# A planner that writes the instruction order by hand: accumulator reads by two engines counted one behind the other, and a larger backlog bound

## The chip, the cores and the metric

The kernel runs on one core of a Trainium2 chip. The metric is device time in microseconds (us) of one execution. Five engines work side by side: TensorE (PE in the profile; its weight loads are PEld), VectorE (DVE), ScalarE (ACT), GpSimd (POOL) and SyncE (SP), which issues most DMAs. Every engine executes its own instructions in the order in which the program issued them.

## The reference

One layer of a decoder for 512 prompt tokens and 8 x 4 sample tokens, all in one matrix of 544 columns, model width 1024, in float32:

```python
hp = _ffn_half(hp, ...)                      # x + 0.5 * SwiGLU(RMSNorm(x)), hidden width 2816
q, k, v, u, gv = _in_proj(_rmsnorm(hp), w_in)  # 8 x 64 | 2 x 64 | 2 x 64 | 512 | 512
q = _rope(q, pos_p)
k = _rope(k, pos_p)
ya = _swa_prompt(q, k, v, sinks)             # window of 128, sinks, blocks of 128 queries
yg = _gmlp(u, gv, ws, b_s)                   # gelu(u) * (tril(W_s) @ RMSNorm(gelu(gv)) + b)
hp = hp + concat(_rmsnorm(ya), _rmsnorm(yg)) @ w_out
hp = _ffn_half(hp, ...)
y = _rmsnorm(hp)
```

The sample tokens take the same path, with attention over a cache of 128 keys each. The last keys, values and gating rows are outputs too.

## The kernel before

Activations lie transposed: 128 features on the partitions, 544 tokens along the free dimension. Each float32 operand is split into a high part (rounded to fp32r) and a low part (the remainder), and a product is three fp32r matmuls: high x high, high x low, low x high. A matmul has 272 columns, half of the tokens. Weights stream in by DMA as `raw` tiles; ScalarE makes the high part `wh`, VectorE the low part `wl`.

Stages in order of time: the first feed-forward block (tiles `aga`, `aua`, `pa_`, `ada`), then the mixing stage in `mix`, then the second feed-forward block (`agb`, `aub`, `pb_`, `adb`) with the final norm. In the mixing stage TensorE's main work is 14 projection tiles of 48 matmuls, in the order k, q0, q1, v, g0, q2, g1, q3, g2, g3, u0 to u3 (accumulators `zk`, `zq`, `zv`, `zg`, `zu`), and then the output projection `o` in two halves of eight tiles: the first needs the attention's result, the second the gating's. Two accumulators turn by turn, with a third one at times, take the tiles.

The other work is side work: Python generators that are advanced in between. They are `unit` (eight attention units of four heads by 128 queries: scores `sp`, softmax in `so`, transposes `tp` to `PT`, product `po`; units 0 to 3 need q0 and q1, units 4 to 7 need q2 and q3), `samples` (`sps`, `srow`, `tps`, `pos`), `outs` (transposes `tpv`, `tpk` of v and k, and their stores), `turn_gv` (transposes `tg`), `y_gen` and `a_stat` (the attention's norm, `R_a`), and `gmlp` (the gating: Gelu of `gv` and `u`, products `mp`, its norm `R_g`). `gmlp` is marked late. In a unit, each `yield` names the tiles and flags that the next piece needs.

The order is written by the program itself, while it is built, with an estimate of time. `Model.put` keeps a clock for each engine (`t`) and, for each tile, a log of accesses with their end times. An instruction starts at the latest of its engine's clock, the accesses that its reads wait for, and the accesses that its writes wait for. `when(box, writes, eng)` gives the end of the latest overlapping access by another engine: with `writes=True` that of writes alone, with `False` that of reads and writes. The estimated costs of each operation are in `Model.op`; for a VectorE operation on two tensors of 544 elements it is 150 + 1.09 x 544 = 743 ns.

After every step of a projection (six matmuls, an eighth of a projection tile) `tick` looks for side work. It returns at once if VectorE's or ScalarE's clock is more than `BACKLOG` ahead of TensorE's. Otherwise it takes the first generator of the list that is `ready`, that is, whose operands are done by TensorE's clock and whose accumulators are free, and advances it until something is issued on TensorE. Late work is taken only where both clocks are less than `BACKLOG / 3` ahead. `force` advances side work without regard to the clocks until a flag is set; the program calls it where the main work needs the side work's result.

An accumulator is read by two engines in the evacuation of k and q, `ev_z`: ScalarE copies it in four pieces into `rot`, and VectorE reads it for `zc` (for k the tile is `kT`). The final norm reads one accumulator (`pRf`) on ScalarE and VectorE too.

```python
for b in range(4):
    nc.scalar.copy(g2(rot[b * 32:(b + 1) * 32, :]), ac[(b ^ 1) * 32:(b ^ 1) * 32 + 32, :, :HT])
zc = kT if kind == "k" else t544(f"zc{i}")
nc.vector.tensor_tensor(g2(zc), ac[:, :, :HT], g2(CR), op=ALU.mult)
nc.vector.tensor_tensor(rot, rot, SR, op=ALU.mult)
```

These two engines' instructions have the framework's semaphores between them; the model's clocks set only in which order the program issues the instructions, and, in `scale`, which of the two engines does a copy.

Of the kernel before, what the change touches and what calls it, by code (L numbers as in the profile page):

```python
# [10 lines left out]
PSUM = bass.MemoryType.PSUM  # L11
# [22 lines left out]
W_BUFS = 5  # L34
NX = 14
SLACK = 4500.0
BACKLOG = 2500.0
MARGIN = 0.0


class Model:
# [22 lines left out]

    def put(self, eng, ns, reads, writes, lat=100.0):
        two = [r for r in reads if len(r.ap) > 1 and r.ap[-1][1] > 1]
        reads, writes = [self.box(r) for r in reads], [self.box(w) for w in writes]
        t = max([self.t[eng]] + [self.when(r, True, eng) for r in reads] + [self.when(w, False, eng) for w in writes])
        if eng == "DVE" and sum(r.space != PSUM for r in two) == 2 and self.pool[0] <= t < self.pool[1]:
            t = self.pool[1]  # L70
        if eng == "POOL":
            self.pool = (t, t + ns)
        self.t[eng] = t + ns - {"DVE": 85.0, "ACT": 95.0}.get(eng, 0.0)
        for bs, w in ((reads, False), (writes, True)):
            for key, *b in bs:
                old = self.log.get(key, [])
                if w:
                    old = [e for e in old if not (b[0] <= e[0] and e[1] <= b[1] and b[2] <= e[2] and e[3] <= b[3])]
                self.log[key] = old[-60:] + [(*b, t + ns + lat, w, eng)]
# [66 lines left out]
class Prog:  # L146
# [34 lines left out]
    def tick(self):  # L181
        if max(self.m.t["DVE"], self.m.t["ACT"]) > self.m.t["PE"] + BACKLOG:
            return
        t = self.m.t["PE"]
        while self.m.t["PE"] == t:
            idle = max(self.m.t["DVE"], self.m.t["ACT"]) < t + BACKLOG / 3
            g = next((g for g in self.side if self.ready(g) and (idle or not g[2])), None)
            if g is None:
                return
            self._advance(g)  # L190
# [1433 lines left out]
```

## Time and profile before

| | us |
|---|---|
| median of 3 runs | 961.84 |
| lowest, highest run | 960.1, 968.4 |
| profiled execution, its own time | 960.9 |
| its span, first to last instruction | 959.2 |
| TensorE busy in the span | 939.2 |
| VectorE busy | 731.0 |
| ScalarE busy | 412.0 |

The mean granted clock of TensorE is 0.992 of full speed. Times in the profile count from the span's start. In the rows of instructions, the first two numbers are start and length in us; `out<-in` names tiles, with buffer numbers left out; `xN` merges N instructions; a bracket gives the idle time of the engine before the instruction and what ended it. Nearly all instructions have line L132, because one helper issues them: they are told apart by their tiles.

### The profile page before, as it was taken

What the parts mean: (1) busy time and instruction counts of PE and PEld (TensorE: products, weight loads), DVE (VectorE), ACT (ScalarE), POOL (GpSimd) and SP (SyncE); (2) the same over time, 40 slices, a digit from 0 to 9 for tenths busy, and PEclk for the clock granted to TensorE, in tenths of its full rate; (3) what the DMA queues carried; (4) which work ended last, traced back from release to release, by engine and by line L of the source; (5) the groups of instructions that cost most, each with busy time, mean ns of one, the idle gap of its engine ahead of it and who ended that gap; (6) DMA issues with size and microseconds to landing.
All of it is one profiled execution on the core that took longest, in us unless ns stands there. A gap on an engine that the chain in (4) does not pass through costs nothing.

```text
span 959.2 us, 18038 instructions
## 1 busy us (share of the span) xinstructions
PE 939.2 (98%) x7463; PEld 927.1 (97%) x7463; DVE 731.0 (76%) x1316; ACT 412.0 (43%) x655; POOL 46.0 (5%) x55
## 2 busy tenths in 40 slices
PE   8999999999999999999999999999999999999996
PEld 7999999999999999989999999999999999999996
DVE  6689996689668957586767796799966799745864
ACT  7434453243424436556546354334442344412432
POOL 0000000000000000130004300000000000000002
PEclk9999999999999999999999999999999999999998
DMA  7321225122422246231131222303242222512202
GB/s 250 121 78 44 90 93 169 65 82 72 144 82 89 77 144 207 67 95 45 67 106 54 73 71 95 104 25 109 78 144 89 87 90 88 177 45 89 88 2 93
DMA packets 29826, 90.86 MB, mean 95 GB/s; under 512 B 3808, under 2 KB 7248, under 8 KB 29600
## 3 DMA queue, kind: packets, MB, share of 16 engines
q1 hardware_dynamic: 28416, 87.85, 28.2%
q0 software_dynamic: 784, 1.30, 0.4%
q8 instruction: 58, 0.95, 0.4%
q10 hardware_dynamic: 544, 0.56, 0.2%
q14 instruction: 24, 0.20, 0.1%
HBM read 86.98 MB, written 3.74 MB: 95 GB/s over the span
## 4 chain that ended last, share of the span: by engine, by line
PE 89%; DVE 5%; ACT 3%; DMA 1%; issue 1%; SPq 0%; POOL 0%; DVEq 0%
PE ada L132 14%; PE adb L132 14%; PE o L132 3%; PE aub L132 3%; PE zu L132 2%; PE agb L132 2%; PE aga L132 2%; PE zg L132 2%; PE aua L132 2%; PE zq L132 1%; DMA x<-x 1%; PE pb_40P L132 1%; PE pa_121P L132 1%; PE pb_161P L132 1%; PE pa_40P L132 1%; PE pa_61P L132 1%
## 5 line engine op out<-in xcount | busy, mean ns | idle before, releaser
L132 ACT ACTIVATE wh<-raw 128x1024 fp32r<-128x1024 f32 (+2 forms) x240 | 220.3, 940 | 262.4 <-DVE raw L132 154.6
L132 DVE TENSOR_TENSOR wl<-raw,wh 128x1024 fp32r<-128x1024 f32 (+2 forms) x240 | 255.6, 1077 | 9.0 <-ACT wh L132 8.7
L132 PE MATMUL adb<-hhb,wh 128*128 128x272 f32 x352 | 78.5, 289 | 0.7 <-DVE hpb L132 0.7
L132 PE MATMUL adb<-hlb,wh 128*128 128x272 f32 x352 | 78.0, 288 | 0.9 <-DVE hlb L132 0.9
L132 PE MATMUL adb<-hhb,wl 128*128 128x272 f32 x352 | 78.1, 288 | 0.0
L132 DVE TENSOR_TENSOR raw<-raw,raw 128x512 f32<-128x512 f32 x108 | 74.2, 687 | 1.3
L132 PE MATMUL ada<-hha,wh 128*128 128x272 f32 x352 | 73.0, 289 | 0.9 <-ACT wh L132 0.9
L132 PE MATMUL ada<-hla,wh 128*128 128x272 f32 x352 | 72.7, 288 | 0.0
L132 PE MATMUL ada<-hha,wl 128*128 128x272 f32 x352 | 72.6, 288 | 0.0
L132 DVE SCALAR_TENSOR_TENSOR x<-adb,x 128x272 f32<-128x272 f32 x64 | 25.9, 436 | 46.8 <-PE adb L132 46.7
L132 PEld LDWEIGHTS adb<-hlb,wh 128*128 128x128 f32 x352 | 57.3, 189 | 1.2 <-DVE hlb L132 1.2
L132 PEld LDWEIGHTS adb<-hhb,wh 128*128 128x128 f32 x352 | 57.4, 188 | 0.9 <-DVE hpb L132 0.9
L132 DVE SCALAR_TENSOR_TENSOR x<-ada,x 128x272 f32<-128x272 f32 x64 | 25.2, 435 | 42.6 <-PE ada L132 42.6
L132 PEld LDWEIGHTS adb<-hhb,wl 128*128 128x128 f32 x352 | 57.1, 189 | 0.0
L132 PEld LDWEIGHTS ada<-hha,wh 128*128 128x128 f32 x352 | 55.2, 188 | 1.1 <-issue 1.1
L132 PEld LDWEIGHTS ada<-hla,wh 128*128 128x128 f32 x352 | 55.4, 189 | 0.0
L132 PEld LDWEIGHTS ada<-hha,wl 128*128 128x128 f32 x352 | 55.2, 189 | 0.0
L132 ACT ACTIVATE hhb<-hpb 128x544 fp32r<-128x544 f32 (+1 forms) x24 | 14.8, 621 | 39.5 <-DVE hpb L132 39.5
L132 ACT ACTIVATE hha<-hpa 128x544 fp32r<-128x544 f32 x22 | 14.5, 659 | 39.2 <-DVE hpa L132 39.2
L132 ACT ACTIVATE xh<-x,cols 128x544 fp32r<-128x544 f32 x24 | 17.8, 749 | 30.4 <-DVE x L132 27.2
L132 PE MATMUL o<-xh,wh 128*128 128x272 f32 x128 | 29.7, 298 | 0.6 <-DVE oa L132 0.6
L132 PE MATMUL o<-xl,wh 128*128 128x272 f32 x128 | 28.5, 289 | 0.1
(818 smaller groups left out, 2821.3 us busy)
## 6 DMA issues: line engine op xcount, KB each, us to landing
raw<-wgu SPq DMA_DIRECT2D x86, 512.0 KB, 3.9
raw<-wd SPq DMA_DIRECT2D x32, 384.0 KB, 3.5
raw<-wd SPq DMA_DIRECT2D x20, 512.0 KB, 4.7
raw<-win SPq DMA_DIRECT2D x14, 512.0 KB, 4.3
raw<-wout SPq DMA_DIRECT2D x8, 512.0 KB, 3.8
x<-x SPq DMA_DIRECT2D x8, 272.0 KB, 4.7
y<-x SPq DMA_DIRECT2D x6, 272.0 KB, 2.4
raw<-wgu SPq DMA_DIRECT2D x8, 128.0 KB, 3.7
```

The costliest lines, as they stand in the source:

```text
L132: return f(*args, **kw)
```

## The change

In `Model.put` a read of an accumulator (a tile in PSUM) now waits, in the estimate, for the reads of it by other engines as well as for the writes. Reads of other memory wait for writes alone, as before. And `BACKLOG` rises from 2500 to 5500 ns, which raises the bound for late work, a third of it, from 833 to 1833 ns. No instruction is added or removed by the edit itself. The order of side work in between the main work can differ, and which engine does the copies that `scale` places.

```diff
-BACKLOG = 2500.0
+BACKLOG = 5500.0
...
         two = [r for r in reads if len(r.ap) > 1 and r.ap[-1][1] > 1]
+        bank = [r.space != PSUM for r in reads]
         reads, writes = [self.box(r) for r in reads], [self.box(w) for w in writes]
-        t = max([self.t[eng]] + [self.when(r, True, eng) for r in reads] + [self.when(w, False, eng) for w in writes])
+        t = max([self.t[eng]] + [self.when(r, b, eng) for r, b in zip(reads, bank)] + [self.when(w, False, eng) for w in writes])
```

## The prediction

> **What bounds the kernel now.** I read the page's totals and chain first, then the waits of TensorE, then the busy time by stage, then the timelines of the one stage where TensorE loses time.
>
> ```profile
> span 959.2 us, 18038 instructions
> PE 939.2 (98%) x7463; PEld 927.1 (97%) x7463; DVE 731.0 (76%) x1316; ACT 412.0 (43%) x655; POOL 46.0 (5%) x55
> PE 89%; DVE 5%; ACT 3%; DMA 1%; issue 1%; SPq 0%; POOL 0%; DVEq 0%
> ```
>
> TensorE (PE) is busy for 939.2 of 959.2 us, and 89% of the chain that ended last is its own. The change removes no matmul, so all it can win is idle or slowed TensorE time. Next, TensorE's waits (us, times, longest), and the stages (stretch, length, busy time and count of PE, PEld, DVE, ACT, POOL, then the granted clock):
>
> ```profile
> PE agb L132 <- DVE xl L132: 1.2, 2, 0.9
> PE sp L132 <- DVE xh L132: 1.0, 1, 1.0
> PE tpv L132 <- DVE vT L132: 0.9, 1, 0.9
> PE o L132 <- DVE oa L132: 0.6, 1, 0.6
> PE sp L132 <- DVE xl L132: 0.3, 1, 0.3
> ...
> 400.00:450.00 50.00, 47.88 (x368) 45.39 (x367) 37.55 (x107) 30.77 (x70) 9.20 (x18) 0.97 0.21 67
> 450.00:500.00 50.00, 49.59 (x404) 46.10 (x405) 33.21 (x108) 25.23 (x72) 1.63 (x2) 1.00 0.24 76
> 560.00:580.00 20.00, 18.82 (x149) 18.38 (x148) 19.83 (x28) 9.72 (x14) 1.04 (x1) 1.00 0.22 69
> 414.00:419.00 5.00, 2.88 (x19) 2.38 (x18) 4.25 (x7) 4.50 (x5) 0.00 (x0) 0.90 0.05 10
> 418.30:422.00 3.70, 3.61 (x19) 3.49 (x20) 3.07 (x14) 0.27 (x1) 0.00 (x0) 0.58 0.69 211
> ```
>
> The planner's side work (attention units, sample attention, gating) lies in the mixing stage, about 385 to 577 us. There 400 to 450 loses most, and nearly all of that is one cluster: 2.12 us idle between 414 and 419, then 3.7 us at a clock of 0.58. The feed-forward blocks have norm statistics as their only side work. That waits for its operand, not for backlog, and no accumulator that precedes it has readers on two engines, so I cost the change at nothing there, with the long matmul runs as cover.
>
> **The estimate (first edit).** Two engines read one accumulator where k and the four q tiles are evacuated: ScalarE copies four rotated pieces, then VectorE multiplies the same accumulator by the cosine table. The three timelines (start, length, instruction, idle time before it and releaser):
>
> ```profile
> 409.34 2.45 ACT L132 COPY rot<-zq 32x544 f32<-32x544 f32 x4
> 411.83 0.72 DVE L132 TENSOR_TENSOR zc<-zq,pre_rope_c 128x544 f32<-128x544 f32 x1 [1.18 <-ACT rot L132]
> 412.47 0.71 DVE L132 TENSOR_TENSOR rot<-rot,pre_rope_s 128x544 f32<-128x544 f32 x1
> 415.55 0.69 DVE L132 TENSOR_TENSOR xl<-zc,xl 64x512 fp32r<-64x512 f32 x1
> 417.62 0.72 DVE L132 TENSOR_TENSOR vT<-zv,R_n 128x544 f32<-128x544 f32 x1
> 419.38 0.28 DVE L132 CUSTOM_DVE_ANT_0 so<-sp,pre_mask_p 128x128 f32<-128x128 f32 x1
> ...
> 411.78 0.41 PE L132 MATMUL zg<-xh,wh 128*128 128x272 f32 x2
> 414.09 0.27 PE L132 MATMUL sp<-KL,xh 128*128 128x128 f32 x1
> 415.37 0.33 PE L132 MATMUL sp<-KH,xh 128*128 128x128 f32 x1 [1.00 <-DVE xh L132]
> 418.39 1.11 PE L132 MATMUL tpv<-ident,vT 128*128 128x128 f32 x4 [0.86 <-DVE vT L132]
> 424.58 0.41 PE L132 MATMUL zq<-xh,wh 128*128 128x272 f32 x2
> ```
>
> The chip does what the new estimate says: the product zc starts at 411.83, when the last of the four copies is done (409.34 + 2.45 = 411.79). The old estimate lets zc run beside the copies, so it sees VectorE free for the next instruction one product early: 412.47 - 411.83 = 0.64 us per tile. Three such tiles (k, q0, q1) precede the first scores, each held by the one before through ScalarE and VectorE in turn, so the old estimate is 3 x 0.64 = 1.9 us early there. The trace fits: the scores of unit 0 (sp) were put in front of TensorE at 414.0, while their last operand, xl of q1, is written at 415.55 + 0.69 = 416.24, 2.2 us later. The new estimate should be off by 2.2 - 1.9 = 0.3 us. The planner looks after every eighth of a tile; the steps here end at 414.03, 414.78, 415.53 and 416.28. So sp moves to 416.28, with 0 to 0.3 us of wait, and the transpose of v (operand at 417.62 + 0.72 = 418.34) to the first step after that. The projection zg0, which waits for neither, fills the time.
>
> What this is worth: from 411.78 to 424.58 TensorE spent 12.80 us. The work in it by undisturbed rows:
>
> ```profile
> 584.96 6.01 PE agb L132 x48
> 465.46 0.84 PE sp L132 x8
> 422.27 0.96 PE sp L132 x8
> ...
> 428.33 0.60 PE L132 MATMUL tp<-ident,so 128*128 128x128 f32 x4
> 428.69 0.50 PE L132 MATMUL zq<-xh,wh 128*128 128x272 f32 x2
> ```
>
> A tile of 48 matmuls 6.01, the scores of two units 0.84 and 0.96, seven transposes at (428.69 - 428.33) / 4 = 0.09, so 0.63: together 8.44 us. Lost: 12.80 - 8.44 = 4.36 us, of which 2.12 are the three waits, 3.70 x (1 - 0.58) = 1.55 the slow clock, and the rest pipeline refills. With 0.36 kept for the remaining error of the estimate, the term is **-4.0 us**. VectorE doesn't pay for it: it is busy until 419.38 either way, where the first softmax read starts in both versions.
>
> [...]
>
> **The backlog (second edit).** At 414.03 VectorE's issued work ends at 419.38, a true lag of 5.35 us, at 416.28 still 3.1. The old estimate saw under 2.5, as it let the step through. With honest lags the old bound of 2.5 would hold sp until 417.03; the new bound of 5.5 doesn't. This alone is worth 0 to 0.75 us in VectorE's start, and I take nothing. In the stages without two-reader tiles (zg, zu, the output projection) the bound really rises by 3 us: steps go in earlier. TensorE has no wait there to lose (0.4 us idle in 450 to 500), so directly this is worth nothing; it is needed to keep the -4.0:
>
> ```profile
> 502.47 0.41 PE L132 MATMUL zu<-xh,wl 128*128 128x272 f32 x2
> 503.18 0.88 DVE L132 TENSOR_SCALAR so<-so,st 128x256 f32<-128x256 f32 x3
> 507.82 0.29 PE L132 MATMUL o<-xh,wh 128*128 128x272 f32 x1
> 509.05 1.08 PE L132 MATMUL po<-PT,vt 128*64 128x256 f32 x8
> 511.70 1.28 ACT L132 ACT_TABLE_LOAD   x1
> 512.99 2.71 ACT L132 ACTIVATE gv<-gv 128x512 f32<-128x512 f32 x5
> 552.91 0.72 DVE L132 TENSOR_TENSOR og<-o,R_g 128x544 f32<-128x544 f32 x1 [3.23 <-ACT R_g L132]
> 575.12 0.78 DVE L132 SCALAR_TENSOR_TENSOR xl<-x,cols,xh 128x544 fp32r<-128x544 f32 x1
> ```
>
> Two places must follow. The output projection starts at 507.82 right behind the last units (po of unit 7 at 509.05); these hang on q3 and zg3, which TensorE now delivers 4 us earlier, and VectorE has room (37.55 and 33.21 busy in two stretches of 50). And the stage's end is VectorE's: once R_g is there, it works from 552.91 to 575.90 with hardly a gap, and the next block waits 1.2 us for its xl. R_g hangs on the gating work, whose Gelu starts at 511.70 as "late" work: the planner admits it only when both engines lag under a third of the bound, 0.83 us before and 1.83 after. At the step that ends at about 502.65 VectorE's lag is 503.18 + 0.88 - 502.65 = 1.4 us: refused before, admitted now. So the Gelu can start up to 9 us earlier; 2.8 (4.0 - 1.2) are enough. The other waits in the list (oa, xl) I take as shuffled, not gone: 0, with -1.8 to +2 as bounds, from their sum and from a cluster like the 2.12 elsewhere.
>
> **Sum.** The profiled execution took 960.9 us (span 959.2 and 1.7 around it); 960.9 - 4.0 = 956.9. The median of the runs shown, 961.84, lies 0.94 higher, so the forecast is **957.8 us**.
>
> **Rivals.**
> - The gain is taken back at the stage's end: the Gelu is not admitted earlier, R_g stays at 552, VectorE's 23 us behind it stay, and TensorE waits for xl. For it: 19.83 busy of 20 in 560 to 580. Against it: the lag of 1.4. Only other losses in the noise go: 961.0.
> [...]
> - Slower: evacuations come too late. Main evacuations queue on VectorE behind side work, which may now lag 5.5 us plus one step. A q tile's evacuation then ends 5.5 + 2.45 + 0.72 = 8.7 us after the tile, while the accumulator is wanted after one more tile, 6.01 plus about 1 us of side matmuls: a wait of 1.7 us. It decides from a lag of about 3.8 us at a tile's end. Four of the nine later tiles at 1.7, two slow-clock stretches at 1.55, less 4.0: +5.9, so 967.7. Against it: at 414 the true lag was 5.35 without such a wait.
> - The order hardly changes, because readiness and not backlog sets it: 961.8.
>
> **How the numbers follow.** Chances: forecast 0.58, gain taken back 0.18, clock 0.05, late evacuations 0.15, no change of order 0.04. All of TensorE's losses between 400 and 577 come to 4.36 + 1.8 + 0.4 = 6.6 us, under 1% (9.6 us, about what a measurement of this kernel can tell from no change), so faster by over 1% gets 0.02. Slower by over 1% (above 971.5) is the upper half of the evacuation case: 0.07. Within 1%: 0.91. The range goes from 961.84 - 6.6 - 1.3 (some noise of the runs) = 954.0 to 966.0, which leaves out the forecast's thin lower end and most of the evacuation case.
>
> **What would show it.** Right: no wait of sp for xh or xl and none of tpv for vT above 0.3 us; a clock of 1.0 from 400 to 450; sp of unit 0 at 416 to 417; zq2 starting near 420.5 instead of 424.58; the Gelu table load before 508; R_g before 549; the wait of agb for xl not longer than 1.2; the same 7463 matmuls. Wrong: new waits of a projection for zc, u or qT (late evacuations), of o for xl or xh (units late), or a longer wait of agb (gain taken back).

## The result, and the profile after

| | before | after |
|---|---|---|
| median, first measurement, us (12 runs of each) | 960.52 | 956.34 |
| ratio to before, 95% interval | | 0.9946 [0.9928, 0.9963] |
| median, second measurement, us (33 and 12 runs) | 961.12 | 954.87 |
| ratio to before, 95% interval | | 0.9940 [0.9921, 0.9959] |
| profiled execution: own time, span, us | 960.9, 959.2 | 956.38, 954.7 |
| its mean granted clock | 0.992 | 0.994 |

The change wins about 0.55%, between 4 and 6 us. The forecast was 957.8 us. Two of the twelve executions of the changed kernel in the first measurement took 1526.67 us (granted clock 0.555) and 2346.97 us; the ratio leaves them out, the median of the ten others is 955.75 us, and since the first profile fell into one of the two, the profile shown here belongs to the second measurement.

The page's totals and chain after:

```profile
span 954.7 us, 18040 instructions
PE 936.6 (98%) x7463; PEld 925.1 (97%) x7463; DVE 729.0 (76%) x1320; ACT 411.4 (43%) x651; POOL 45.7 (5%) x55
PE 91%; DVE 4%; ACT 2%; DMA 1%; issue 1%; SPq 0%; POOL 0%; DVEq 0%
```

The same 7463 matmuls; four instructions went from ScalarE to VectorE. TensorE's waits after (total us, times, longest):

```profile
PE pss_n L133 <- DVE ss L133: 2.2, 1, 2.2
...
PE tpv L133 <- DVE vT L133: 0.9, 1, 0.9
...
PE o L133 <- DVE oa L133: 0.6, 1, 0.6
...
PE o L133 <- DVE u L133: 0.4, 1, 0.4
PE po L133 <- DVE PT L133: 0.3, 1, 0.3
```

The waits of `sp` (1.0 and 0.3) and that of `agb` for `xl` (1.2) are gone. The wait of `tpv` for `vT` is still there. The stages after (stretch, length, busy time and count by engine, granted clock, DMA share, GB/s):

```profile
400.00:450.00 50.00, 48.80 (x386) 46.21 (x385) 36.69 (x103) 33.11 (x73) 9.13 (x18) 1.00 0.21 67
450.00:500.00 50.00, 50.00 (x410) 46.06 (x409) 34.11 (x116) 26.73 (x73) 1.74 (x3) 1.00 0.24 76
560.00:580.00 20.00, 20.00 (x164) 20.00 (x163) 16.12 (x22) 8.81 (x13) 2.10 (x1) 1.00 0.31 99
414.00:419.00 5.00, 4.14 (x33) 3.80 (x33) 4.18 (x8) 4.42 (x5) 0.00 (x0) 1.00 0.05 17
```

400 to 450 rose from 47.88 to 48.80 of 50 at a clock of 1.00, and 560 to 580 from 18.82 to 20.00 of 20. So the time came from two places, the cluster and the stage's end. Both in the timelines (start, length, instruction, idle time before it):

```profile
409.88 2.46 ACT L133 COPY rot<-zq 32x544 f32<-32x544 f32 x4
412.37 0.72 DVE L133 TENSOR_TENSOR zc<-zq,pre_rope_c 128x544 f32<-128x544 f32 x1 [1.19 <-ACT rot L133]
416.09 0.69 DVE L133 TENSOR_TENSOR xl<-zc,xl 64x512 fp32r<-64x512 f32 x1
418.16 0.72 DVE L133 TENSOR_TENSOR vT<-zv,R_n 128x544 f32<-128x544 f32 x1
...
412.32 0.41 PE L133 MATMUL zg<-xh,wh 128*128 128x272 f32 x2
416.07 0.22 PE L133 MATMUL sp<-KH,xh 128*128 128x128 f32 x1
416.84 0.33 PE L133 MATMUL sp<-KH,xl 128*128 128x128 f32 x1
418.94 0.66 PE L133 MATMUL tpv<-ident,vT 128*128 128x128 f32 x4 [0.86 <-DVE vT L133]
422.20 0.41 PE L133 MATMUL zq<-xh,wh 128*128 128x272 f32 x2
...
498.80 1.28 ACT L133 ACT_TABLE_LOAD   x1
548.39 0.72 DVE L133 TENSOR_TENSOR og<-o,R_g 128x544 f32<-128x544 f32 x1 [3.55 <-ACT R_g L133]
566.44 0.41 PE L133 MATMUL agb<-xh,wh 128*128 128x272 f32 x2
570.51 0.78 DVE L133 SCALAR_TENSOR_TENSOR xl<-x,cols,xh 128x544 fp32r<-128x544 f32 x1
```

The cluster from zg0 to zq2 takes 422.20 - 412.32 = 9.88 us instead of 12.80. The scores `sp` come 416.07 - 412.32 = 3.75 us behind zg0's start instead of 2.25 (414.03 in the profile before): two steps of six matmuls later. The Gelu's table load went from 511.70 to 498.80, the first product with `R_g` from 552.91 to 548.39, and the last `xl` starts at 570.51 instead of 575.12.

Milestones of TensorE (first matmul of a tile, us) show where the gain lies. The rows "again" are second profiles of the same two kernels, told of below; the last two columns are differences within a row.

| | zk | zg0 | zq2 | agb | adb | zg0 to zq2 | agb to adb |
|---|---|---|---|---|---|---|---|
| before | 385.23 | 411.78 | 424.58 | 568.82 | 620.88 | 12.80 | 52.06 |
| before, again | 382.98 | 409.52 | 420.93 | 565.15 | 617.17 | 11.41 | 52.02 |
| after | 385.77 | 412.32 | 422.20 | 566.44 | 616.79 | 9.88 | 50.35 |
| after, again | 385.89 | 412.44 | 422.35 | 566.62 | 616.97 | 9.91 | 50.35 |

From zq2 to agb all four take the same, 144.22 to 144.27 us. The cluster gave 2.92 us in the first pair of profiles, and the first 50 us of the second feed-forward block 1.71.

### The profile page after: what moved, and what is told of

Its sections match the earlier page's. It is cut to its first block, busy times and chain, and to the rows that moved or that the text cites. A ratio compares the mean times of both kernels' runs of the same rounds, so it can differ in the third digit from the quotient of the medians.

```text
span 1525.0 us, 18040 instructions
## 1 busy us (share of the span) xinstructions
PE 1513.2 (99%) x7463; PEld 1457.2 (96%) x7463; DVE 743.6 (49%) x1320; ACT 419.6 (28%) x651; POOL 44.9 (3%) x55
## 4 chain that ended last, share of the span: by engine, by line
PE 99%; DVE 0%; DMA 0%; ACT 0%; issue 0%; SPq 0%; DVEq 0%; ACTq 0%
PE ada L133 14%; PE adb L133 14%; PE o L133 5%; PE zg L133 3%; PE aga L133 3%; PE zu L133 3%; PE aub L133 3%; PE zq L133 3%; PE aua L133 3%; PE agb L133 3%; PE pb_181P L133 1%; PE pb_60P L133 1%; PE pb_161P L133 1%; PE pb_121P L133 1%; PE pb_81P L133 1%; PE pa_160P L133 1%
## 5 line engine op out<-in xcount | busy, mean ns | idle before, releaser
L133 PE MATMUL adb<-hhb,wh 128*128 128x272 f32 x352 | 111.8, 395 | 0.6 <-DVE hpb L133 0.6
L133 PE MATMUL adb<-hhb,wl 128*128 128x272 f32 x352 | 111.2, 394 | 0.0
L133 PE MATMUL adb<-hlb,wh 128*128 128x272 f32 x352 | 111.1, 394 | 0.0
L133 PE MATMUL ada<-hha,wh 128*128 128x272 f32 x352 | 105.2, 394 | 0.9 <-DVE hpa L133 0.9
L133 PE MATMUL ada<-hha,wl 128*128 128x272 f32 x352 | 105.4, 395 | 0.0
L133 PE MATMUL ada<-hla,wh 128*128 128x272 f32 x352 | 105.3, 394 | 0.0
L133 PEld LDWEIGHTS ada<-hha,wh 128*128 128x128 f32 x352 | 75.7, 232 | 3.2 <-ACT wh L133 1.3
L133 PEld LDWEIGHTS ada<-hla,wh 128*128 128x128 f32 x352 | 76.0, 233 | 1.9
L133 PEld LDWEIGHTS ada<-hha,wl 128*128 128x128 f32 x352 | 75.7, 232 | 2.0
L133 PE MATMUL o<-xh,wl 128*128 128x272 f32 x128 | 39.9, 387 | 0.0
```

Of the source, the lines that this page charges most:

```text
L133: return f(*args, **kw)
```

## Experiments

Theory at the outset: the estimate moves `sp` and `tpv` behind their operands, and the higher bounds keep what that wins. Rivals: the bound alone does it; the bound is not needed; the gain is really one of the clock. All ratios are against runs of the kernel before on the same chip. The whole change, each edit alone and the late bound of 833 ran on one chip (before: 961.12 us), the thin filler, the two other bounds and the later norm on a second (960.42), the rest on a third (960.54).

**The whole change.** The kernel after, unaltered, for its profile and a second measurement.

> The changed kernel once more, with an undisturbed profile. Theory (cluster): about 4 us under the kernel before (ratio 0.995 to 0.997); no wait of sp for xh or xl and of tpv for vT above 0.3 us, a granted clock of 1.0 from 400 to 450 us, zq2 starts near 420.5 us instead of 424.58. Rival (chance shuffle: the gain is a sum of small differences all over the mixing stage): the cluster at 414 to 422 is still there in part, and 1 us or more is gained elsewhere.

954.87 us, ratio 0.9940 [0.9921, 0.9959]. Its profile is the one above. The waits of `sp` are gone and the clock is 1.00 from 400 to 450, as expected. The wait of `tpv` stayed, zq2 came at 422.20 instead of near 420.5, and 1.7 us were gained elsewhere, as the rival had it in part.

**Each edit alone.**

```diff
# new estimate, old bounds
-BACKLOG = 5500.0
+BACKLOG = 2500.0
# old estimate, new bounds (against the kernel before)
-BACKLOG = 2500.0
+BACKLOG = 5500.0
```

> First edit alone: the new estimate with the backlog bound left at 2500. Theory: the cluster at 414 to 422 goes as in the full change (-4 us there), but side work is held back by the honest lags; units 6 and 7 are issued only at the start of the output projection, by force, and TensorE waits there for softmax and transposes: 2 to 6 us back, so 958 to 963 in all, not faster than the full change. Rival (the estimate alone carries the gain, the bound does nothing): 956 to 957, as the full change.

> Second edit alone: backlog bound 5500 with the old estimate. Theory: the scores of unit 0 go one step earlier still, so TensorE waits 0.7 us longer for xh and xl (about 2.0 us in all for sp) and the slow clock stays: 961 to 962, 0 to 1.5 us slower than before. Rival (the bound carries the gain): 957 to 958.

The estimate alone: 968.55 us, ratio 1.0077 [1.0049, 1.0104], slower than before and slower than the 958 to 963 expected. Its waits in the mixing stage, and the stretch where the output projection begins:

```profile
PE tp L133 <- ACT so L133: 2.9, 1, 2.9
PE o L133 <- DVE xl L133: 2.5, 3, 1.7
PE mp L133 <- DVE kT L133: 1.8, 1, 1.8
PE o L133 <- DVE oa L133: 1.1, 1, 1.1
...
500.00:520.00 20.00, 15.88 (x123) 13.49 (x120) 13.23 (x42) 12.36 (x28) 1.90 (x2) 1.00 0.12 40
```

The cluster is as short as with the whole change (9.92 us), but with honest lags the old bound holds side work back, and the rows read as if units 6 and 7 were forced through where the output projection needs them (`tp` is issued 2.9 us ahead of its operand): TensorE is busy for 15.88 of 20 us, and `agb` comes 573.15 - 383.93 = 189.2 us behind zk, where the whole change has 566.44 - 385.77 = 180.7 and before 183.6.

The bounds alone: 963.14 us, ratio 1.0027 [1.0008, 1.0045], where 961 to 962 were expected. `sp` now comes a step earlier still:

```profile
PE o L132 <- DVE oa L132: 2.4, 1, 2.4
PE sp L132 <- DVE xh L132: 1.8, 1, 1.8
PE tpv L132 <- DVE vT L132: 0.9, 1, 0.9
```

The bounds alone do take away the wait of `agb` (agb to adb 50.34 us, as with the whole change), but from zq2 to agb they lose 3.8 us (148.07 instead of 144.2). Neither edit is worth anything alone; together they gain.

**Which bound.** The whole change with the late work's bound as before (833 ns), then with the bound for all side work as before (2500 ns) and late work's at 1833, then with 8000 for all side work and 1833 for late work.

```diff
# late bound old
-            idle = max(self.m.t["DVE"], self.m.t["ACT"]) < t + BACKLOG / 3
+            idle = max(self.m.t["DVE"], self.m.t["ACT"]) < t + 2500.0 / 3
# side bound old (late bound stays 5500 / 3)
-        if max(self.m.t["DVE"], self.m.t["ACT"]) > self.m.t["PE"] + BACKLOG:
+        if max(self.m.t["DVE"], self.m.t["ACT"]) > self.m.t["PE"] + 2500.0:
# bound 8000 (late bound stays 5500 / 3)
-BACKLOG = 5500.0
+BACKLOG = 8000.0
```

> The full change, but the bound for late work left at 833 ns instead of a third of 5500. Theory: the cluster goes as in the full change; the gating work starts later, so R_g is later and TensorE waits for xl at the start of the next block: 1 to 3 us of the 4 are taken back, 957.5 to 959.5. Rival (the stage's end does not hang on the gating's start): 956 to 957, no difference from the full change.

> The full change, but the bound for all side work left at 2500 ns; only the bound for late work is the new one (1833 ns). Theory (the side bound is what the new estimate needs): units 6 and 7 come out by force at the start of the output projection as with the estimate alone; TensorE waits there 2 to 5 us and the clock may fall: 961 to 968, not faster than before. Rival (the late bound carries the gain): 955 to 957.

> The new estimate with the side bound at 8000 instead of 5500 and the late bound kept at 1833. Theory (from 5500 on readiness sets the order, the bound hardly acts): within 1.5 us of the full change, 954 to 957. Rival (late evacuations, from more backlog): new waits of the projections for zc, u or qT, 958 or more.

| | median, us | ratio [95%] |
|---|---|---|
| late bound 833 | 957.16 | 0.9957 [0.9934, 0.9980] |
| side bound 2500 | 965.26 | 1.0047 [1.0028, 1.0066] |
| side bound 8000 | 957.20 | 0.9958 [0.9941, 0.9975] |

The expectations were 957.5 to 959.5, 961 to 968 and 954 to 957; the first and the third median lie 0.3 and 0.2 us outside. With the late bound at 833, the Gelu comes 3.83 us later than with the whole change, the product with `R_g` 3.03 us, and the wait of `agb` is back:

```profile
PE agb L133 <- DVE xl L133: 1.1, 2, 0.8
...
502.63 1.28 ACT L133 ACT_TABLE_LOAD   x1
551.42 0.72 DVE L133 TENSOR_TENSOR og<-o,R_g 128x544 f32<-128x544 f32 x1 [3.24 <-ACT R_g L133]
```

So the gain at the stage's end needs the new bound for late work: without it agb to adb takes 51.99 us instead of 50.35, and the median is 957.16 - 954.87 = 2.3 us higher. Yet the Gelu's time is not what decides there. `R_g` hangs on a matmul `rb_g` that broadcasts it, before and after:

```profile
551.05 1.20 PE L132 MATMUL rb_g<-ident,rs_g 128*128 128x128 f32 x10
...
546.53 1.20 PE L133 MATMUL rb_g<-ident,rs_g 128*128 128x128 f32 x10
```

It stands 568.82 - 551.05 = 17.8 us ahead of agb before, and 566.44 - 546.53 = 19.9 with the whole change, 18 matmuls of the output projection earlier. With the late bound at 833 and with 8000 it stands 17.8 us ahead, as before (549.56 to 567.35 and 549.36 to 567.13), though the Gelu comes 9 and 11 us earlier than before (502.63 and 500.25 instead of 511.70). With the side bound at 2500 the wait of `tp` at the start of the output projection comes back:

```profile
PE tp L133 <- ACT so L133: 2.9, 1, 2.9
```

The larger bound for side work is what the estimate needs, and without it the gain becomes a loss. With 8000 nothing is gained over 5500: no projection waits for `zc`, `u` or `qT`, and `agb` waits 1.1 us for `xl` again. The new bound for late work is needed for the gain at the end, but doesn't secure it.

**Filling the waits.** Is the slow clock at 418 to 422 us made by the waits ahead of it? Two kernels with the order of before, in which TensorE runs matmuls without use in the first and the last wait, into parts of accumulators that are overwritten afterwards: first ten thin ones, then seventeen of full width.

```diff
# thin: 6 before the first scores, 4 before the transposes of v
+self.tc.nc.tensor.matmul(sp[:, 1, 256:384], self.ident, self.ident, start=True, stop=True)
+self.tc.nc.tensor.matmul(tp[:, 0:128], self.ident, self.ident, start=True, stop=True)
# full width: 10 and 7
+self.tc.nc.tensor.matmul(sp[:, 1, 0:HT], self.xh[:, 0, 0:128], self.xh[:, 1, 0:HT], start=True, stop=True)
+self.tc.nc.tensor.matmul(tp[:, 0:HT], self.xh[:, 0, 0:128], self.xh[:, 1, 0:HT], start=True, stop=True)
```

> The kernel before, in its own order, with ten extra matmuls on a constant in the two waits: six ahead of the scores of unit 0 and four ahead of the transposes of v, into accumulators that the real work overwrites. They take about the time that TensorE waits there anyway. Theory (the slow clock is the work of these waits): the clock in 418 to 422 goes from 0.58 to 1.0 although the operands come no earlier; 1 to 2 us under the kernel before (ratio 0.998 to 0.999) and a mean clock nearer 0.995. Rival (the clock falls on its own there): 0.58 stays, the time is that of the kernel before or up to 0.5 us more.

> The kernel before, with ten and seven matmuls of 272 columns without use put into the first and the last wait of the cluster at 414 to 419 us (they write parts of accumulators that are overwritten afterwards), so that TensorE works there at full width where the earlier filler was thin. If the slow clock after the cluster comes from these waits, it is gone in the profile (418 to 422 at 1.00) and, in 12 runs, the mean granted clock rises from 0.9916 to about 0.995 and the time falls by 1 to 2 us, ratio about 0.998. If the clock falls on grounds of its own, the ratio is about 1.000 and the mean clock stays at 0.9916, as with the thin filler.

| | median, us (12 runs) | ratio [95%] | mean clock of the runs; of before's |
|---|---|---|---|
| thin | 961.39 | 1.0008 [0.9988, 1.0029] | 0.9916; 0.9917 |
| full width | 960.19 | 0.9993 [0.9975, 1.0010] | 0.9925; 0.9914 |

In the profile with the thin ones the slow stretch is gone:

```profile
418.30:422.00 3.70, 3.70 (x33) 3.67 (x32) 3.64 (x19) 0.51 (x4) 0.78 (x2) 1.00 0.76 236
```

Alone, that row would have looked like a proof. The runs don't show what was expected: neither filler changes the time or, measurably, the mean clock. Nor do they rule a smaller effect out. A slow stretch as in the profile before (3.41 us at a clock of 0.50, from 417.99 to 421.40) costs by estimate at most 1.7 us and 0.0018 of the mean clock, the second profile of that kernel, below, has none there, and the intervals reach 2 us to either side. The profile with the full-width filler shows why a single profile misleads. It has a clock of 1.00 at 418 to 422, and a slow stretch at another place:

```profile
480.00:485.00 5.00, 5.00 (x49) 4.30 (x48) 1.00 (x3) 0.00 (x0) 0.00 (x0) 0.88 0.01 3
485.00:490.00 5.00, 5.00 (x22) 4.00 (x21) 2.99 (x7) 2.90 (x10) 0.10 (x1) 0.50 0.75 233
...
483.07 1.27 PE L132 MATMUL pos<-sT,kcv 128*64 128x16 f32 x16
484.27 0.82 PE L132 MATMUL zu<-xh,wh 128*128 128x272 f32 x2
```

TensorE is busy for 10.00 of 10 us there, and from 430 to 490 its longest wait is 0.2 us. Ahead of the slow stretch stand transposes (`tg`, `tp`, 472 to 479) and narrow matmuls (`pos`, 16 columns) among the projection's: a pair of the projection's matmuls takes 0.82 us at 484.27 instead of 0.41 with no wait in sight.

**Both kernels once more.** One more profile of each, for what recurs.

> The kernel before, unchanged, one more profile. If the slow clock at 418 to 422 us belongs to the waits of the cluster, it is there again with the same three waits (1.00, 0.26, 0.86) and a clock near 0.58. If it falls on grounds of its own, the waits are there again and the slow slices lie elsewhere, or nowhere.

> The full change, one more profile. The waits (tpv for vT 0.86, none of sp, none of agb for xl) depend on the order alone and should come again to a tenth of a us, with the milestones of the stage (second q tile 36.4 us behind the stage's start, the second feed-forward block's down projection 231 us behind it). If slow slices follow from particular waits, they lie where the first profile had them (20 to 30 and 940 to 950 us); if not, elsewhere.

The kernel before, again (957.21 us in this execution, clock 0.995), its waits and the stretches around the cluster:

```profile
PE sp L132 <- DVE xh L132: 1.0, 1, 1.0
...
PE tpv L132 <- DVE vT L132: 0.9, 1, 0.9
...
PE sp L132 <- DVE xl L132: 0.3, 1, 0.3
...
410.00:420.00 10.00, 7.89 (x62) 7.36 (x61) 9.08 (x28) 4.92 (x7) 0.67 (x2) 1.00 0.40 123
420.00:430.00 10.00, 10.00 (x82) 9.47 (x81) 7.82 (x34) 6.04 (x22) 8.53 (x17) 1.00 0.29 95
...
409.52 0.41 PE L132 MATMUL zg<-xh,wh 128*128 128x272 f32 x2
420.93 0.41 PE L132 MATMUL zq<-xh,wh 128*128 128x272 f32 x2
```

The same three waits, and no slow clock behind them. So the cluster takes 12.80 us with the slow stretch and 11.41 without it; the stretch costs 1.39 us where it falls. With the change it is 9.88 (9.91 in the second profile of the kernel after). What the order alone is worth there is 11.41 - 9.88 = 1.53 us.

The kernel after, again (956.23 us, clock 0.996), has the same waits and milestones as its first profile, as expected: zk to zq2 36.46 us (36.43), zk to adb 231.08 (231.02). Its slow stretch lies where the first had it, behind the wait of `pss_n` (25.82 to 29.23 us; 25.41 to 28.82). These two second profiles are only 1.0 us apart in total, because zk comes 2.9 us later in that of the kernel after. TensorE's order up to there is the same in both kernels, so this is a difference between executions.

**Beyond the change.** The first block's norm waits 2.2 us for its operand (`pss_n`) in both profiles of the kernel after and in the first of before (0.6 in the second). The full change with these statistics 2.3 us later in the planner's eyes; and besides that with the transpose of v 0.9 us later, to take away the wait of `tpv`.

```diff
# norm later
-        yield [ss[:, t0:t1], "tr"]
+        ok = self.m.when(self.m.box(ss)) + 2300.0 if tag == "n1" else 0.0
+        yield [ss[:, t0:t1], "tr", lambda: self.m.t["PE"] >= ok]
# besides: v later
-                yield [vT, "tr"]
+                ok = self.m.when(self.m.box(vT)) + 900.0
+                yield [vT, "tr", lambda: self.m.t["PE"] >= ok]
```

> The full change plus one edit outside it: the first block's norm statistics are issued three projection steps later, when their operand is really there. Theory (a wait of 2.2 us and the slow clock behind it, 0.64 for 4.7 us in the kernel before, are the same pattern as in the mixing stage): the wait of pss_n goes to under 0.5 us and the clock from 20 to 30 to 1.0; 1.5 to 4 us under the full change, 951 to 954. Rival (the reciprocal root and its broadcast are late next, and the accumulators wait for them): 955 to 957, with a new wait of the up projection in its place.

> The full change with the norm statistics of the first block 2.3 us later, as before, and besides the transpose of v 0.9 us later than the planner thinks its operand ready, since the full change still has a wait of 0.86 us there. Theory (the estimate is still 0.9 us early for v, and that is what the forecast's larger term missed): the wait of tpv for vT goes, the second q tile starts 0.5 to 1 us earlier against the stage's start (35.5 to 36 instead of 36.4), and the median falls from 952.7 to about 952. Rival (what is won there is lost at the next wait, since the order of all later side work moves): second q tile earlier, but the median is 952.5 to 955.

Norm later: 952.72 us (6 runs), ratio 0.9919 [0.9899, 0.9939], the lowest median of all and inside the 951 to 954 expected. That it is faster than the plain change is not shown: the two ran on different chips, and their intervals overlap. The wait of `pss_n` is gone, the clock from 20 to 30 us is 1.00, and a shorter wait is new:

```profile
PE aua L133 <- DVE sa L133: 1.4, 1, 1.4
```

With v later besides: 968.24 us (6 runs), ratio 1.0070 [1.0057, 1.0083]. The wait of `tpv` did go. The cluster took 8.11 us instead of 9.91, but unit 1's scores (0.94 us) now come behind zq2; with them it is 9.05, and the 0.86 us less are the wait. Unit 0's transposes missed a place and came at 427.87 instead of 423.56, the fifth unit's scores at 469.07 instead of 459.56, and TensorE waits for the last units again:

```profile
PE o L133 <- DVE xl L133: 3.1, 1, 3.1
PE po L133 <- DVE PT L133: 1.9, 1, 1.9
PE tp L133 <- ACT so L133: 1.9, 2, 1.4
...
500.00:510.00 10.00, 6.61 (x32) 4.69 (x30) 6.96 (x17) 5.55 (x15) 0.00 (x0) 0.66 0.16 52
```

A wait of 0.86 us was taken away, and the median is 15.5 us higher; zk to agb takes 194.98 us instead of 180.50. The expectation was wrong, its rival's price of up to 3 us too: all side work behind the moved step is placed anew, and the last units find no place before the output projection.

## Why the prediction was right or wrong

The median lay 1.5 us under the forecast in the first measurement and 2.9 in the second, inside the range and with less than 1% of gain, as forecast. That the number came so near is in part luck, as the steps show:

- **The estimate's remaining error** was mis-sized: forecast 0.3 us, measured 0.7 to 0.8. `sp` was put in front of TensorE at 416.07, and its last operand was written at 416.09 + 0.69 = 416.78. It moved by two steps, not three; this cost under 0.2 us, because six of its eight matmuls don't need that operand. The transpose of v was ready to go at 418.94 - 0.86 = 418.08, when `vT` lacked 418.16 + 0.72 - 418.08 = 0.80 us. That its wait would go was wrong: 0.86 before, 0.86 after. A possible reason, not tested: the 2.2 us were read off the step at which `sp` was issued, but the planner looks only every 0.75 us, so its estimate may have been up to 0.75 us earlier still.
- **The term -4.0** was mis-sized accordingly. It came to -2.92 between the first two profiles, of which 1.39 is the slow stretch (forecast 1.55) and 1.53 the order. zq2 starts at 422.20, not near 420.5. The slow stretch was absent behind the same waits in the second profile, so counting it in full, from one profile's row, was the error. That the slow clock is not the work of these waits at all (the chance of 0.05 called clock) is not borne out either: by the count in the last section, 17 of 18 stretches with as few columns as these waits leave had half the clock behind them, and no other stretch had. The mean price of the waits' slow stretch is an estimated 0.7 us, less than half of the 1.55. The 0.69 us that the sum calls pipeline refills no run shows as such; what is left beside the undisturbed work, the waits and the slow stretch is 11.41 - 8.44 - 2.11 = 0.86 us in the second profile of the kernel before and 9.88 - 8.44 - 0.86 = 0.58 after.
- **Other waits "shuffled, not gone: 0"** failed at the stage's end. The wait of `agb` for `xl` (1.2 us) went, and with it the stretch from agb to adb fell by 1.71 us. A mechanism for it was in the text, as a condition for keeping the cluster's gain: the Gelu admitted earlier by the late bound. The 2.8 us that were called enough don't come out: a wait of 1.2 us is a lack and no reserve, so with TensorE 4.0 us earlier `R_g` had to come 4.0 earlier to keep that wait and 5.2 to end it. TensorE reached agb 2.38 us earlier, so 3.6 would end it, and `R_g` came 4.52 earlier. The Gelu itself moved 12.90 us, but its time doesn't set `R_g` alone: with the old late bound and with 8000 it moved 9 and 11 us, and the wait stayed. What counted is the place of `rb_g` in TensorE's order, and the sum had no term for it.
- **The backlog "directly nothing, but needed"** was right, and its price was far too low. Without the larger side bound the change isn't back at 961.0 but at 965 to 969 us. The prediction saw the first scores held for 0.75 us and not the last units late at the output projection.
- **Feed-forward blocks at nothing** was right for all but the first 50 us of the second: zk comes at 385.77 instead of 385.23, where two profiles of the kernel before have 385.23 and 382.98, and from adb to the end it takes 337.91 us instead of 338.32.
- **Rivals.** Late evacuations: no wait of this kind, even at a bound of 8000. Gain taken back at the stage's end: the opposite happened. That the order hardly changes: it changes (`sp` by two steps, `rb_g` by 18 matmuls).

The errors partly cancel: 1.1 us too much at the cluster, 1.7 too little at the end; with the 0.54 later at zk and the 0.41 less behind adb, the profiled time fell by 4.5 us where 4.0 were forecast. What the order and what the clock has of the gain over many runs is worked out in the last section.

## What to carry to other kernels

Correct a planner's cost model and its thresholds together: a bound that let work through under flattering estimates can be too tight for honest ones, and each of the two edits alone was slower here. Judge a moved step by the last work that it pushes, not by the wait that it removes: 0.86 us won at 415 cost 15 us behind it. And before a slow clock in one profile goes into a sum, look whether a second profile of the same kernel has it at the same place, and if not, weigh it by how often it can fall there.

## What the runs showed of the hardware

The mean granted clock differs from run to run of one kernel, and the time with it. Over 77 runs of the kernel before, from 956.76 us at 0.995 to 967.11 at 0.986, a straight line gives 8.6 us per 0.01 of clock, with a correlation of -0.90. The kernel after has a mean clock of 0.9952 in 13 runs, before 0.9916. A fit with one slope for both puts 2.7 us (+-0.7) of the 5.8 us between their means on the order and 3.1 on the clock; the clean profiles give 1.53 + 1.67 = 3.2 us for the order. So, by this fit, about half of the gain is clock. The variants whose last units come late at the output projection have a lower clock (0.9885, 0.9897, 0.9877), which by that line makes up an estimated 1.7 to 3.2 us of their loss. But filling the cluster's waits did not raise it measurably. What in the new order raises the clock by 0.0036 stays open for the greater part; the cluster accounts for some 0.0008 of it, by the estimate that follows.

What stands ahead of a slow stretch can be counted in the traces. In each of the 13 profiles used here all changes of the granted clock lie whole multiples of 3.41 us apart, and the clock of a slow stretch is 0.50. In the profile before they come at 25.46, 28.87, 417.99, 421.40 and 950.47 us, which is 1, 114, 1 and 155 times 3.413 us from each to the next; with the full-width filler one slow stretch goes from 483.85 to 490.67. These steps lie at other places in other executions: the first slow stretch starts at 25.46 us in the profile before, at 25.41 and 25.82 in the two of the kernel after. The count is of the stretch of one step, 3.41 us, just ahead of a change. Four rows: before (ahead of the slow stretch, and the slow stretch), before again, full-width filler (ahead of its slow stretch):

```profile
414.58:417.99 3.41, 1.91 (x12) 1.55 (x12) 3.23 (x6) 3.34 (x5) 0.00 (x0) 1.00 0.00 0
417.99:421.40 3.41, 3.01 (x14) 2.89 (x15) 2.92 (x11) 0.58 (x1) 0.00 (x0) 0.50 0.65 191
...
413.46:416.87 3.41, 2.30 (x17) 1.94 (x17) 3.35 (x5) 2.83 (x3) 0.00 (x0) 1.00 0.07 26
...
480.44:483.85 3.41, 3.41 (x40) 2.90 (x40) 0.28 (x1) 0.00 (x0) 0.00 (x0) 1.00 0.02 5
```

An undisturbed projection takes 6.01 / 48 = 0.125 us for 272 columns, so it streams about 7416 columns in 3.41 us. The matmuls that start in the first row have 2400 columns together (32% of that), in the third 3072 (41%), in the fourth 2480 (33%): TensorE is busy throughout the fourth, but its matmuls are narrow. Of some 3500 such stretches at full clock between 8 and 935 us in the 13 profiles, 18 have under 37%. Seventeen of these were followed by half the clock, the eighteenth (32%, in the run of the estimate alone) was not, and no other stretch was. This is a count over these traces and not an experiment. By it, about half of all places of the 3.41 us steps (1.62 of 3.41 us, with the rows of "before, again") put so thin a stretch into the cluster, hence the estimate of 0.47 x 1.39 = 0.7 us and 0.47 x 0.0018 = 0.0008 of the clock. No place does in the kernel after (43% at the least) or with either filler (53% and 63%).

The same three waits had 0.58 behind them (418.30 to 422.00) in one profile of the kernel before and 1.00 in the other (410.00 to 430.00). The stretch at 485 to 490 with the full-width filler has a clock of 0.50 with TensorE's longest wait before it, from 430 on, at 0.2 us. There, from 472 to 484, transposes and narrow matmuls stand among the projection's; the unchanged kernel has them too, from 470 to 485, at 1.00 in its second profile. In that one the 3.41 us steps cut them into two stretches of 54% each, where the filler's profile has 33% in one. No run here tells the transposes' part in this from that of the narrow matmuls.
